# A two-layer decoder trunk: the feed-forward and the second mixer begin by tile of tokens, and the norm's scale and shift move to VectorE

## The chip, the core and the metric

The kernel runs on one core of a Trainium2 chip. The core's engines run side by side and wait for each other through semaphores: TensorE (PE, matrix products; PEld is its weight loading), VectorE (DVE), ScalarE (ACT), GpSimd (POOL), and SyncE (SP), which here only issues DMAs. Each engine takes its instructions strictly in the order in which they are written. The metric is device time in microseconds (us) of one execution. The profile below is of one execution; its times are counted from its first instruction.

## What is computed

256 tokens with 1024 features pass through two layers. Cut to what matters here, the reference is

```python
for l in range(2):
    sh1, sc1, g1, sh2, sc2, g2 = split(c_act @ w_ada[l] + b_ada[l])
    h = x * (1.0 + sc1) + sh1
    mix = hybrid_mixer(h, w_in[l], ...)        # four branches, gates, w_out
    x = layer_norm(alpha * x + g1 * mix, ln1_g[l], ln1_b[l])
    h = x * (1.0 + sc2) + sh2
    f = swiglu(h, ...) if l == 0 else moe(h, ...)
    x = layer_norm(alpha * x + g2 * f, ln2_g[l], ln2_b[l])
```

A layer norm is a mean and a variance over the 1024 features of a token, a normalisation, and then a scale and a shift per feature (`ln_g`, `ln_b`). The next sub-layer needs the norm's result in two forms: as `h`, turned so that features lie on the partitions, for the next products; and as `x`, for the next residual sum.

## The kernel before

**Products.** All weights are fp32 and pass through the core once. A weight chunk of 1 MB (128 x 2048 numbers) is fetched by SyncE into one of three `raw` buffers. Each of its halves (128 x 1024) is split: ScalarE copies it into `whi` in the format fp32r (line 303), and VectorE subtracts that copy from the raw half into `wlo` (line 306). There are five buffers of each. The moving side is split in the same way (`hhi`, `hlo`), and every product is made of three: hi times hi (line 383), lo times hi (384), hi times lo (385). `half` writes the work of one weight half: it splits up to three halves ahead, finishes earlier results (`flush`), writes the products and then lets one step of the side work run (`step`, on the list `tasks`; the heads of the mixer, for instance, are such tasks). The order in which the program is written is the order on each engine; there is no other scheduler.

**Two joints.** There are two places where a layer norm stands between two sub-layers and the kernel goes straight on with products of the result: in layer 0 between the mixer's last projection (`project`) and the feed-forward (`ffn`), called **joint 1** here, and between the feed-forward's second matrix and layer 1's mixer, called **joint 2**. The 256 tokens are two tiles of 128, `x[0]` and `x[1]` ("tile 0" and "tile 1"). `by_token` writes the last four weight halves ahead of a joint so that tile 0 is finished first: its 512 remaining columns (part 0), then tile 1's in two quarters of 256 (parts 1 and 2, woven). After each part `ln_last` writes the sums and the norm's statistics (`ln_part`), and behind the last of a tile the normalisation in place (`ln_fin`, two VectorE instructions at line 542 after a power on GpSimd at line 535).

**What `ln_last` does at the end.** All behind part 2: TensorE turns tile 0 (`transposes`, line 565), then come the two products of a gate row (`row_end`, line 496), then tile 1's turns. `modulate` makes `h` out of the turned tile: eight ScalarE instructions with scale and shift (line 574), the split's copy by ScalarE for tile 0 (line 580) and by VectorE for tile 1 (line 578), and VectorE's subtraction (line 581). Only then `ffn` or the mixer writes its first products, and each of them streams both tiles (256 columns of `h`).

**Scale and shift.** After that `ln_affine` writes four GpSimd instructions of 128 x 1024 (lines 590 and 591) which bring `x` to its final form, with rows that a GpSimd-issued DMA has spread over the partitions. `x` is next read at the next residual sum, many weight halves later.

Layer 1's mixer begins with the chunks of `xbc` (for the state-space branch), then takes the list `PLAN`, in which `bv` is third. `EXTRA` names halves after which one more step of the side work runs.

## Time and profile before

| | |
|---|---|
| time, median of 3 runs | 1923.5 us (1922.97 to 1925.78) |
| the profiled execution's own time | 1922.38 us |
| its span, first to last instruction | 1920.6 us |
| TensorE busy | 1864.4 us, 97% of the span |
| VectorE, ScalarE, GpSimd busy | 1603.2, 1191.6 and 211.5 us |
| layer 0's mixer, joint 1, feed-forward | to 370.9, 370.9 to 410, 410 to 568.7 us |
| joint 2, layer 1's mixer, its projection, experts | 568.7 to 600, 600 to 925, 925 to 942, 942 to 1900 us |

TensorE is the busy engine, so time is gained where it stands still or runs at the lower of its two clocks; the busy time of other engines matters only where TensorE ends up waiting for them. Matrix products overlap in the engine, so a product's row shows a duration that is longer than the distance to the next row; the distance is the cost.

### The profile page before, as it was taken

How to read it: one execution, taken by the hardware profiler on the slowest of the kernel's cores; microseconds unless marked ns; L12 is line 12 of the kernel's file. 1: busy time of each engine (PE TensorE's matmuls, PEld its weight loads, DVE VectorE, ACT ScalarE, POOL GpSimd, SP SyncE). 2: the span in 40 equal slices, each digit the busy share in tenths (PEclk: the TensorE clock that was granted, in tenths of full speed). 3: DMA queues.
4: the chain of work that ended last, by engine and by line, in shares of the span. 5: the costliest groups of instructions: out<-in, count | busy, mean ns of one | idle time of the engine just before them, and what ended most of it. 6: DMA issues, size and time to landing. Idle time of an engine off the chain costs nothing.

```text
span 1920.6 us, 29039 instructions
## 1 busy us (share of the span) xinstructions
PE 1864.4 (97%) x11206; PEld 1629.3 (85%) x11206; DVE 1603.2 (83%) x1995; ACT 1191.6 (62%) x1505; POOL 211.5 (11%) x209
## 2 busy tenths in 40 slices
PE   6999999999999999999999999999999999999997
PEld 5888989899989889999888888888888888888885
DVE  7776876887757686766898998999989999899997
ACT  4546534545435446444577777777777777777774
POOL 0023332110003133321000000000000000000000
PEclk9999999999999999999999999999999999999999
DMA  9565665477845465655899999999999999999992
GB/s 354 190 256 207 233 228 216 153 276 277 302 153 202 160 231 213 237 203 181 337 370 346 345 371 376 380 378 353 369 375 383 378 351 371 349 406 384 381 403 110
DMA packets 86740, 566.00 MB, mean 295 GB/s; under 512 B 10177, under 2 KB 10433, under 8 KB 24642
## 3 DMA queue, kind: packets, MB, share of 16 engines
q1 hardware_dynamic: 82226, 550.30, 75.9%
q0 software_dynamic: 4224, 13.65, 2.0%
q8 instruction: 90, 1.47, 0.3%
q14 instruction: 56, 0.46, 0.1%
q10 hardware_dynamic: 144, 0.11, 0.0%
HBM read 557.21 MB, written 6.82 MB: 294 GB/s over the span
## 4 chain that ended last, share of the span: by engine, by line
PE 89%; DVE 4%; issue 2%; DMA 2%; ACT 1%; POOL 1%; SPq 0%; DVEq 0%; POOLq 0%; ACTq 0%
PE mm L383 22%; PE mm L385 22%; PE mm L384 22%; PE mx L384 6%; PE mx L385 6%; PE mx L383 6%; PE mx L1446 1%; DVE wlo L306 1%; DMA raw<-in_win_dram 1%; PE mx L667 1%; PE mx L1313 1%; ACT h L574 1%; DMA w<-in_cst_dram 1%; DMA raw<-in_adaT_dram 1%; DVE raw L439 0%
## 5 line engine op out<-in xcount | busy, mean ns | idle before, releaser
L306 DVE TENSOR_TENSOR wlo<-raw,whi 128x1024 fp32r<-128x1024 f32 (+1 forms) x880 | 1047.2, 1233 | 196.9 <-ACT whi L303 195.1
L303 ACT ACTIVATE whi<-raw 128x1024 fp32r<-128x1024 f32 (+1 forms) x880 | 879.9, 1051 | 136.1 <-DMA raw<-in_win_dram 29.9
L383 PE MATMUL mm<-hhi,whi 128*128 128x256 f32 x1376 | 393.3, 286 | 16.4 <-ACT whi L303 12.7
L385 PE MATMUL mm<-hhi,wlo 128*128 128x256 f32 x1376 | 386.7, 281 | 7.8 <-DVE wlo L306 7.7
L384 PE MATMUL mm<-hlo,whi 128*128 128x256 f32 x1376 | 386.5, 281 | 0.5 <-DVE hlo L581 0.3
L383 PE MATMUL mm<-whi,ghi 128*128 128x512 f32 x896 | 350.3, 391 | 0.0
L385 PE MATMUL mm<-whi,glo 128*128 128x512 f32 x896 | 349.0, 390 | 0.0
L384 PE MATMUL mm<-wlo,ghi 128*128 128x512 f32 x896 | 348.7, 389 | 0.0
L383 PEld LDWEIGHTS mm<-hhi,whi 128*128 128x128 f32 x1376 | 264.0, 192 | 25.4 <-ACT whi L303 14.8
L385 PEld LDWEIGHTS mm<-hhi,wlo 128*128 128x128 f32 x1376 | 263.8, 192 | 8.7 <-DVE wlo L306 8.7
L384 PEld LDWEIGHTS mm<-hlo,whi 128*128 128x128 f32 x1376 | 264.0, 192 | 1.6 <-DVE hlo L581 1.0
L385 PEld LDWEIGHTS mm<-whi,glo 128*128 128x128 f32 x896 | 168.2, 188 | 35.9
L384 PEld LDWEIGHTS mm<-wlo,ghi 128*128 128x128 f32 x896 | 168.2, 188 | 34.9 <-DVE wlo L306 0.2
L383 PEld LDWEIGHTS mm<-whi,ghi 128*128 128x128 f32 x896 | 168.2, 188 | 34.3
L383 PE MATMUL mx<-whi,ehi 128*128 128x512 f32 x448 | 179.6, 401 | 0.0
L385 PE MATMUL mx<-whi,elo 128*128 128x512 f32 x448 | 175.1, 391 | 0.0
L384 PE MATMUL mx<-wlo,ehi 128*128 128x512 f32 x448 | 174.9, 390 | 0.0
L392 ACT ACTIVATE ehi<-mx 128x512 fp32r<-128x512 f32 x56 | 33.6, 600 | 112.9 <-PE mx L1446 112.9
L1406 POOL DMA_INDIRECT outs<-lnt,row x14 | 14.3, 1025 | 807.0 <-DVE lnt L1400 804.9
L385 PEld LDWEIGHTS mx<-whi,elo 128*128 128x128 f32 x448 | 84.0, 188 | 18.0
L384 PEld LDWEIGHTS mx<-wlo,ehi 128*128 128x128 f32 x448 | 84.3, 188 | 16.5 <-DVE wlo L306 0.8
L383 PEld LDWEIGHTS mx<-whi,ehi 128*128 128x128 f32 x448 | 84.2, 188 | 15.7
(359 smaller groups left out, 2456.1 us busy)
## 6 DMA issues: line engine op xcount, KB each, us to landing
raw<-in_egu_dram SPq DMA_DIRECT2D x205, 1024.0 KB, 7.4
raw<-in_edn_dram SPq DMA_DIRECT2D x96, 1024.0 KB, 7.5
raw<-in_win_dram SPq DMA_DIRECT2D x79, 1024.0 KB, 4.9
raw<-in_adaT_dram SPq DMA_DIRECT2D x31, 1024.0 KB, 5.3
raw<-in_fgu_dram SPq DMA_DIRECT2D x22, 1024.0 KB, 4.9
raw<-in_adaR_dram SPq DMA_DIRECT2D x16, 1024.0 KB, 4.9
raw<-in_wbr_dram SPq DMA_DIRECT2D x16, 1024.0 KB, 4.9
raw<-in_fdn_dram SPq DMA_DIRECT2D x11, 1024.0 KB, 5.8
```

The costliest lines, as they stand in the source:

```text
L303: act.activation(hi[:, c], raw, AF.Copy)
L306: dve.tensor_sub(lo[:, c], raw, hi[:, c].bitcast(F32))
L383: pe.matmul(ps, a[0], b[0], start=start, stop=False, **kw)
L384: pe.matmul(ps, a[0], b[1], start=False, stop=False, **kw)
L385: pe.matmul(ps, a[1], b[0], start=False, stop=stop, **kw)
L392: act.activation(hi, src, AF.Copy)
L574: act.activation(h32[:, j], pts[kh][:, j * 128:(j + 1) * 128], AF.Identity, scale=A[:, k:k + 1], bias=B[:, k:k + 1])
L667: pe.matmul(o[64 * j:64 * j + 64, :], v[:, 0, 128 * p + 64 * j:128 * p + 64 * j + 64], ws[j][:, 0:256], start=True, stop=False, skip_group ...
L1313: pe.matmul(o, xs[t][part][:, k * P:(k + 1) * P], dsp[:, t].rearrange("p a b -> p (a b)"), start=(n == 0), stop=(n == 3))
L1406: nc.gpsimd.indirect_dma_start(outs[c][:, :], bass.IndirectOffsetOnAxis(ap=row[:, 0:1], axis=0), y, None)
L1446: pe.transpose(pt[:, k * P:(k + 1) * P], g[:, k * P:(k + 1) * P], ident)
```

## The change

Before, the order behind a joint was: finish both tiles' norm, turn both, make both tiles of `h`, then products of both. The change interleaves the tiles.

- `by_token` splits one more weight half early, and `ln_last` turns tile 0 ahead of the last twelve products (part 2), and writes tile 0's `modulate` behind part 1.
- The buffers of `h` at joint 1 are new (`h1`), because the old ones still hold the projection's input at that time.
- Tile 1 is normalised by one ScalarE instruction of 128 x 1024 (scale and bias per token) instead of two on VectorE.
- The feed-forward's first pair of chunks and layer 1's `bv`, which becomes the mixer's first projection, go through `token_first`: 24 products of 512 columns for tile 0, then 24 for tile 1, with the four weight halves kept for both. Tile 1's turns stand between tile 0's second and third weight half (`rest`).
- The feed-forward's first pair of chunks is packed the other way round (tokens on the partitions), so its result is turned back by two transposes for each tile.
- `ln_affine` becomes a task: eight VectorE instructions of 128 x 512 in steps of the side work, in layer 0 among the feed-forward's halves, in layer 1 behind all other tasks of the mixer. The GpSimd instructions are gone; GpSimd still issues the DMAs of the rows.

```diff
+    o["fgu"][0:2] = gu[:, :, :, :, 0].transpose(0, 2, 1, 3, 4, 5).reshape(2, P, 2048)
...
+            add(win[i] for i in WIN_N["bv"][0])
             add(win[i] for q in WIN_T["xbc"] for i in q)
...
+                if hold:
+                    assert h == 0 and len(src) == 1
+                    held.append(lambda: dve.tensor_sub(lo, raw, hi.bitcast(F32)))
+                else:
+                    dve.tensor_sub(lo[:, c], raw, hi[:, c].bitcast(F32))
...
+    def token_first(fs, rest, end):
+
+        q = state["done"]
+        for i in range(4):
+            split_upto(q + i)
+            flush()
+            split_upto(q + 3)
+            for f in fs(0, i, *parts[q + i]):
+                f()
+            next(rest, None)
+            step()
+        end(0)
+        for i in range(4):
+            flush()
+            for f in fs(1, i, *parts.pop(q + i)):
+                f()
+            state["done"] += 1
+            split_upto(q + 4 + i)
+            step()
+        end(1)
...
+                if i == 0 and early:
+                    split_upto(q + HALVES)
...
-    def ln_last(pss, grow, AB):
+    def ln_last(pss, grow, AB, new):
+
+        R = {}
+
+        def rest(row, mv):
+            next(row)
+            yield
+            m = modulate(R["hT"], 1, transposes(1), *AB)
+            for _ in m:
+                pass
+            yield
 
         def end(part):
             ln_part(pss[part], grow, *PART[part])
-            if part != 1:
-                ln_fin(PART[part][0])
-            if part == 2:
-                hT = state["hT"] = new_hT()
-                modulate(hT, 0, transposes(0), *AB)
-
+            if part == 0:
+                ln_fin(0)
+            elif part == 1:
+                R["hT"] = state["hT"] = new()
+                R["m"] = modulate(R["hT"], 0, transposes(0), *AB)
+                next(R["m"])
+                split_upto(state["done"] + HALVES - 1, hold=True)
+                next(R["m"])
+            else:
                 row = state.pop("row")
                 next(row)
-                modulate(hT, 1, transposes(1), *AB)
-                next(row)
+                mv = ln_stat(1)
+                dve.scalar_tensor_tensor(mv[:, 4:5], mv[:, 0:1], -1.0, mv[:, 3:4], op0=ALU.mult, op1=ALU.mult)
+                act.activation(x[1], x[1], AF.Identity, scale=mv[:, 3:4], bias=mv[:, 4:5])
+                held.pop()()
+                for _ in R["m"]:
+                    pass
+                state["rest"] = rest(row, mv)
         return end
...
-    def ln_affine(g, b):
-        for t in range(2):
-            pool.tensor_tensor(x[t], x[t], g, op=ALU.mult)
-            pool.tensor_tensor(x[t], x[t], b, op=ALU.add)
+    def ln_affine(l, i, wait=0):
+
+        for _ in range(wait):
+            yield
+        for j, op in ((i, ALU.mult), (i + 1, ALU.add)):
+            cl = [slice(c * 512, (c + 1) * 512) for c in range(2)]
+            rows = [rowp.tile([P, 512], F32, name="lnt", bufs=2) for _ in range(2)]
+            for cs, row in zip(cl, rows):
+                nc.gpsimd.dma_start(row, I["lnp"][l, j:j + 1, cs].to_broadcast([P, 512]))
+            yield
+            for cs, row in zip(cl, rows):
+                yield
+                for t in range(2):
+                    dve.tensor_tensor(x[t][:, cs], x[t][:, cs], row, op=op)
+                    for _ in range(min(wait, 2)):
+                        yield
...
+    def first_N(a, rest, end):
+        pss = [bank() for _ in range(2)]
+        token_first(lambda t, i, hi, lo: [mm3(pss[t], sub(a, A_, 2 * i + k, slice(t * 128, t * 128 + 128)),
+                                              sub((hi, lo), A_, slice(k * 512, (k + 1) * 512)),
+                                              i == 0 and k == 0, i == 3 and k == 1) for k in range(2)],
+                    rest, lambda t: end(pss, t))
...
+        if l == 1:
+            tasks.append(ln_affine(0, 2))
...
+            T["bv"] = proj_N("bv", state.pop("rest"))
...
+        first_N(hT, state.pop("rest"), first)
+        for f2 in range(1, nf // 2):
...
+                h = fp.tile([P, 112 + 4096 + 16], F32R, name="h1")[:, 112:112 + 4096].rearrange("p (i k t) -> p i k t", i=2, k=8)
+                return h[:, 0], h[:, 1]
...
-                ln_affine(lnrow(l, 0, fp), lnrow(l, 1, fp))
+                tasks.append(ln_affine(l, 0, 8))
                 ffn(hT, fp, after_ffn)
...
-WFF = 2, 2
+WFF = 3, 2
-EXTRA = (24, 44, 45, 46), (46, 56)
+EXTRA = (24, 44, 45, 46), (38, 42, 46, 52, 56, 72)
```

The order on three engines at joint 1 follows, before and after (line numbers of the changed kernel are its own; its products stand at lines 417 to 419 and its splits at 310 and 317). First TensorE, from the last products of the projection to the first of the feed-forward; `cst` is the identity matrix of the turns, `x_87` and `x_88` are tiles 0 and 1, `acc` and `one` make the gate row. Before:

```order
L383 MATMUL mx<-whi,hhi 128x256
L384 MATMUL mx<-wlo,hhi 128x256
L385 MATMUL mx<-whi,hlo 128x256
L565 MATMUL mx<-cst,x_87 128x128 x8
L496 MATMUL mx<-acc,one 128x512 x2
L565 MATMUL mx<-cst,x_88 128x128 x8
L383 MATMUL mm<-hhi,whi 128x256
L384 MATMUL mm<-hlo,whi 128x256
L385 MATMUL mm<-hhi,wlo 128x256
```

After (twelve products stand behind the first turns, and twelve between the gate row and the second):

```order
L617 MATMUL mx<-cst,x_87 128x128 x8
L417 MATMUL mx<-whi,hhi 128x256
L418 MATMUL mx<-wlo,hhi 128x256
...
L530 MATMUL mx<-acc,one 128x512 x2
L417 MATMUL mm<-whi,h_3996 128x512
L418 MATMUL mm<-wlo,h_3996 128x512
...
L617 MATMUL mx<-cst,x_88 128x128 x8
```

Tile 0's turns moved ahead of the projection's last twelve products, and tile 1's moved behind the feed-forward's first twelve.

Next ScalarE at the same place; `h_...` are the modulated tiles on their way, `grow` is the gate row. Before:

```order
L303 ACTIVATE whi<-raw 128x1024 x6
L574 ACTIVATE h_4024<-mx,b0B,b0A 128x128 x4
L580 ACTIVATE hhi<-h_4024 128x4x128
L574 ACTIVATE h_4031<-mx,b0B,b0A 128x128 x4
L580 ACTIVATE hhi<-h_4031 128x4x128
L574 ACTIVATE h_4053<-mx,b0B,b0A 128x128 x4
L574 ACTIVATE h_4060<-mx,b0B,b0A 128x128 x4
L501 ACTIVATE grow<-mx 128x512 x2
L303 ACTIVATE whi<-raw 128x1024 x5
```

After:

```order
L626 ACTIVATE h_4007<-mx,b0B,b0A 128x128 x4
L632 ACTIVATE h_3996<-h_4007 128x4x128
L310 ACTIVATE whi<-raw 128x1024
L626 ACTIVATE h_4017<-mx,b0B,b0A 128x128 x4
L632 ACTIVATE h_3996<-h_4017 128x4x128
L605 ACTIVATE x_88<-x_88,lmv 128x1024
L310 ACTIVATE whi<-raw 128x1024
L535 ACTIVATE grow<-mx 128x512 x2
L626 ACTIVATE h_4086<-mx,b0B,b0A 128x128 x4
L626 ACTIVATE h_4093<-mx,b0B,b0A 128x128 x4
L1217 ACT_TABLE_LOAD
```

Two weight copies, tile 1's normalisation and the gate row now stand between the two tiles' modulations.

Last GpSimd, from joint 1's power (`lmv`) to the next layer's accumulator. Before:

```order
L535 TENSOR_TENSOR lmv<-lmv,nhalf 128x1 x2
L585 DMA lnrow<-in_lnp_dram 128x1024 x2
L590 TENSOR_TENSOR x_87<-x_87,lnrow 128x1024
L591 TENSOR_TENSOR x_87<-x_87,lnrow 128x1024
L590 TENSOR_TENSOR x_88<-x_88,lnrow 128x1024
L591 TENSOR_TENSOR x_88<-x_88,lnrow 128x1024
```

After:

```order
L569 TENSOR_TENSOR lmv<-lmv,nhalf 128x1 x2
L646 DMA lnt<-in_lnp_dram 128x512 x4
L506 MEMSET acc 128x1024
L508 DMA acc<-in_bada_dram 1x16x64
L569 TENSOR_TENSOR lmv<-lmv,nhalf 128x1 x2
```

The four large instructions are gone from GpSimd; joint 2's power is five rows away.

## Rows read from the trace of the kernel before

**Rows 1.** Windows by stage: length, busy us (instructions) by engine, granted clock, DMA.

```profile
370.89:410.00 39.11, 32.13 (x228) 29.99 (x227) 34.01 (x41) 21.20 (x37) 14.46 (x9) 0.87 0.55 197
410.00:568.66 158.66, 158.66 (x1195) 150.77 (x1194) 114.08 (x147) 69.17 (x94) 0.56 (x1) 1.00 0.71 257
600.00:925.00 325.00, 322.11 (x2494) 297.12 (x2493) 239.36 (x376) 159.84 (x238) 76.11 (x68) 1.00 0.58 212
```

**Rows 2.** Timeline of TensorE, joint 1: start, us, instruction, count, idle before and releaser.

```profile
366.81 0.28 PE L383 MATMUL mm<-whi,hhi 128*128 128x256 f32 x1
...
372.25 1.03 PE L565 MATMUL mx<-cst,x 128*128 128x128 f32 x8
373.12 1.88 PE L496 MATMUL mx<-acc,one 128*128 128x512 f32 x4
...
379.02 0.38 PE L383 MATMUL mm<-hhi,whi 128*128 128x256 f32 x1 [1.86 <-DVE hhi L578]
...
388.38 0.58 PE L385 MATMUL mm<-hhi,wlo 128*128 128x256 f32 x1 [3.90 <-DVE wlo L306]
```

**Rows 3.** Timeline of TensorE, joint 2.

```profile
562.91 0.28 PE L383 MATMUL mm<-whi,fhi 128*128 128x256 f32 x1
...
568.66 1.03 PE L565 MATMUL mx<-cst,x 128*128 128x128 f32 x8
...
584.78 0.42 PE L385 MATMUL mm<-hhi,wlo 128*128 128x256 f32 x1 [2.99 <-DVE wlo L306]
```

**Rows 4.** Timeline of VectorE, joint 1.

```profile
362.20 1.21 DVE L306 TENSOR_TENSOR wlo<-raw,whi 128x1024 fp32r<-128x1024 f32 x1
...
370.26 1.00 DVE L542 TENSOR_SCALAR x<-x,lmv 128x512 f32<-128x512 f32 x2 [0.67 <-POOL lmv L535]
...
372.45 0.42 DVE L522 TENSOR_TENSOR lnt<-mx,grow 128x256 f32<-128x256 f32 x1
...
374.93 1.00 DVE L542 TENSOR_SCALAR x<-x,lmv 128x512 f32<-128x512 f32 x2 [0.68 <-POOL lmv L535]
...
378.54 0.43 DVE L578 CAST hhi<-h 128x512 fp32r<-128x512 f32 x1 [0.70 <-ACT h L574]
...
384.97 7.81 DVE L306 TENSOR_TENSOR wlo<-raw,whi 128x1024 fp32r<-128x1024 f32 x3
```

**Rows 5.** Instructions that read `lnrow`, whole run: ns min/median/max, first and last start.

```profile
L590 POOL TENSOR_TENSOR x<-x,lnrow x4: 2384/2772/2802, 379.2 to 580.9; 128x1024 f32<-128x1024 f32 x4
L591 POOL TENSOR_TENSOR x<-x,lnrow x4: 2464/2855/3243, 382.0 to 583.7; 128x1024 f32<-128x1024 f32 x4
```

**Rows 6.** Timeline of ScalarE, joint 1 to the first result of the feed-forward.

```profile
372.89 1.51 ACT L574 ACTIVATE h<-mx,b0B,b0A 128x128 f32<-128x128 f32 x4 [10.08 <-PE mx L565]
374.43 0.63 ACT L580 ACTIVATE hhi<-h 128x512 fp32r<-128x512 f32 x1
...
379.75 1.12 ACT L501 ACTIVATE grow<-mx 128x512 f32<-128x512 f32 x2
380.70 3.00 ACT L303 ACTIVATE whi<-raw 128x1024 fp32r<-128x1024 f32 x3
...
399.19 0.38 ACT L1147 ACTIVATE fg<-mm 128x256 f32<-128x256 f32 x1
```

**Rows 7.** Timeline of ScalarE, joint 2, second result of the mixer's first unit.

```profile
594.64 0.60 ACT L699 ACTIVATE pad<-mm 128x512 f32<-128x512 f32 x1 [0.26 <-PE mm L385]
```

**Rows 8.** Windows of TensorE alone: length, busy us (instructions), granted clock, DMA.

```profile
82.00:83.00 1.00, 0.00 (x0) 1.00 0.00 0
286.00:288.00 2.00, 0.39 (x1) 1.00 1.00 332
288.00:290.00 2.00, 1.27 (x5) 0.51 0.92 385
```

**Rows 9.** Timelines of VectorE and of GpSimd behind joint 2.

```profile
589.10 2.35 DVE L306 TENSOR_TENSOR wlo<-raw,whi 128x1024 fp32r<-128x1024 f32 x2
...
589.42 0.54 POOL L1188 DMA_DIRECT2D outs<-lnt  x1
```

## What I predict, and why

> **What bounds the kernel now.** I read the busy times first: TensorE works almost through the whole span, so only its pauses and slow stretches are to be had. The windows by stage say where these are: the feed-forward proper has no pause at all, layer 1's mixer has 2.9 us in 325, and joint 1 has 7 us of idle time in 39 at a mean granted clock of 0.87, that is with a stretch at the lower of its two levels, 1.2 instead of 2.4 GHz [rows 1]. Then I read joint 1 on TensorE's timeline. The reader is to see three things there: tile 0's turns begin at 372.25 right behind the last product, the first product of the feed-forward begins only at 379.02, waiting for VectorE's copy of tile 1's `h`, and 26 products later there is a pause of 3.9 us for a `wlo` [rows 2]. Joint 2 has the same shape, with 3.0 us [rows 3].
>
> Why `wlo` is late is seen on VectorE: alone, the subtraction takes 1.21 us; the three that begin at 384.97 take 7.81, or 2.6 each [rows 4]. In that time GpSimd works on its four scale-and-shift instructions of 2.4 to 3.2 us (eight in the run, four behind each joint) [rows 5]. So each joint pays for a serial chain (norm, turn, modulate, for both tiles) and for VectorE being slowed beside GpSimd.
>
> **How much is to be had.** A product of 256 columns costs 0.113 us (48 from 366.81 to 372.25 [rows 2]), one of 512 twice that, 0.23. The first unit behind joint 1 is 96 products of 256 columns, 10.9 us; with turns (0.87 twice, 372.25 to 373.12) and gate row (1.88) [rows 2] that is 14.5 us of work. It ran from 372.25 to 398.9 (ScalarE takes its last result at 399.19, 0.3 later [rows 6]), or 26.6 us. Joint 2: 568.66 [rows 3] to 594.4 [rows 7], 25.7 us. So 12.1 and 11.2 us are lost, 23.3 in all. This is the most that the change can give at the joints.
>
> **Joint 1 after the change, step by step.** Nothing moves before tile 1's first quarter is done, twelve products before 372.25, at 370.9.
>
> TensorE: `x[0]` is normalised in two instructions from 370.26 [rows 4], so the turns run 370.9 to 371.8, the last twelve products to 373.15, the gate row to 375.05.
>
> ScalarE begins 0.64 after the turns, as it did (372.25 to 372.89 [rows 2, 6]): four modulations 371.55 to 373.05 (1.51), copy to 373.7 (0.63), a weight copy to 374.7 (1.0), four modulations to 376.2, copy to 376.8 [rows 6].
>
> VectorE: behind `x[0]` at 371.2 the early `wlo` to 372.4, then tile 1's first quarter, three steps of 0.46, to 373.8; tile 0's first `hlo`, 512 wide (0.7, from 1.21 for 1024), to 374.5; second quarter, aggregate and GpSimd's power as before 2.5 us (372.45 to 374.93 [rows 4]), to 377.0; one small product more, 377.1; the held `wlo` to 378.3; `hlo` to 379.0.
>
> Tile 1 is normalised on ScalarE from 377.15 to 378.2 (1.05, the price of a 1024-wide copy). Then a weight copy to 379.25 and the gate row, 1.12 [rows 6], to 380.4.
>
> TensorE has tile 0's first twelve products at hand at 375.05 and is through at 377.8. It waits 0.5 us for `x[1]`, turns it until 379.2, and does the other twelve by 381.95 (the last `wlo` is there at 380.5). Tile 1's modulations are done by 381.9 and 383.4 on ScalarE, the copies and subtractions on VectorE (0.43 [rows 4] and 0.7) at 382.4, 383.1, 383.9, 384.6. TensorE waits another 0.5 and 0.2 us and then runs 24 products with a turn of tile 0's result (0.2) to 388.4.
>
> So the unit ends at 388.4 instead of 398.9: **10.5 us**, less 0.2 for the second turn-back, **10.3**. What hides the chain is tile 0's own products: if they weren't there, tile 1's modulations from 380.4 would all stand on the path. What is late next is ScalarE, unbroken from 371.55 to 383.4, and then the table load. Behind it the weight copies for the next unit are ready at 386 and 387, in time for 388.4, and the chunk for the fourth one is fetched when the second is split, at about 388.6, eleven us ahead of its products at about 399.5.
>
> **Joint 2.** The same steps from 567.2 (twelve products of 0.12 us before 568.66 [rows 3]). No turn-back is needed, `bv` is wanted with tokens on the partitions. With the same 17.5 us the unit ends at 584.7 instead of 594.4: **9.7 us**.
>
> **Scale and shift.** GpSimd's eight instructions go, and with them VectorE's slow stretches, already counted above. VectorE gets 16 instructions of 512 columns, 0.7 us each or 5.6 us per layer. In the feed-forward it is busy 114 of 158.7 us and in the mixer 239 of 325 [rows 1]; at the rate of one or two per weight half (2.7 us of products) they fit. They wait for rows fetched by GpSimd's queue, and behind them on VectorE the next `wlo` is queued; but the rows are asked for at least one half ahead. I put this at 0; if each stood on the path it would be 11.2 us.
>
> **The rest.** Layer 1's mixer starts `xbc` four halves later, and its tasks get eight steps more. I put that at 0, between -2.9 (all its idle time gone) and the price of the second rival.
>
> A rule bears on joint 2. Beside a DMA issue of GpSimd, two subtractions took 2.35 us [rows 9], no more than alone. The Trainium skill, "SBUF — State Buffer", section "Who interferes with whom", says that a copy or cast on VectorE can enter a two-port mode that holds a port pair shared with GpSimd, and that whichever comes second waits for the whole of the other. The change puts the eight clearing DMAs of the mixer close to tile 1's two casts; by the rule each cast could wait for one issue (0.54 us [rows 9]), and joint 2 would give 8.6 instead of 9.7 us. No run here shows a cast there, and I leave it out.
>
> **Sum.** 10.3 + 9.7 = 20.0 us. I take off 1 us for some twenty hand-overs between engines that I rounded away: 19.0. The profiled execution took 1922.4 us (span 1920.6), 1.1 below the median of 1923.5; against the median this gives **1904.5 us**. A measurement of this kernel can tell about 0.2%, 3.8 us, from no change.
>
> **Rivals.**
> *The clock falls at the joints all the same.* Against it: a pause of 1.1 us left the clock at its upper level [rows 8], and mine are 0.5. For it: with 0.39 us of work between 286 and 288 it fell [rows 8], and turns and gate row stand close to my pauses. Joint 1's mean of 0.87 over 39 us is 10 us at half speed, 5 us lost [rows 1]; kept at both joints, 10 us: 1914.5. Chance 0.10.
>
> *A branch in layer 1's mixer isn't ready.* The state-space and stick-breaking heads begin four halves later (4 x 2.7 = 10.9 us); if the added steps don't make up for that, `flush_to` writes their remaining steps without products between them, and TensorE pauses. At most the whole delay comes back: 1915. For it: the heads are long chains through four engines. Against: idle time there is only 2.9 us now [rows 1], and eight steps are added for six used. Chance 0.09.
>
> *The place of `h1`.* Products cost 0.113 us in the projection, but 48 of them cost 5.75 us, 0.120 each, with `fhi` [rows 2, 3]: where the operands lie seems to matter. The feed-forward streams `h1` in 960 products; at 0.120 it would lose 6.2 us: 1910.7, chance 0.05. This is also how it ends slower: from 0.139 us on (20.0 + 3.8 us over 960 products) the change costs more than it gives. At 0.142, a quarter above the dearest row here, 1930 us. No row has such a price; chance 0.02.
>
> *The change does nothing.* Tile 1's chain could be so late that TensorE waits for it as before. It would have to lose 17 of 20 us, four times the ScalarE chain between 377 and 381. Chance 0.04; 1922.
>
> **How the numbers follow.** My own case has 0.70: from 1900 (the full 23.3 us) to 1909 (two us more lost at each joint). The range goes on to 1912.5 to take in a clock that falls at one joint only, and the mild form of the third rival; outside stay the first two rivals at full price, the last two cases, and little below. Faster by over 0.2%: 0.94; within: 0.04; slower: 0.02.
>
> **What would show it.** Right: no TensorE pause above 1 us at either joint; granted clock at 1.00 through both; no VectorE subtraction of 1024 columns above 1.3 us there; the end of the first unit 17 to 18 us after tile 1's first quarter. Wrong: a wait for `x[1]` or tile 1's `h` of 2 us or more; half clock behind 382; pauses in layer 1's mixer above 5 us; products of the feed-forward at 0.12 us apart.

## The result, and the profile after

The changed kernel takes 1905.5 us (median of 4 runs, 1901.95 to 1908.61) against 1924.3 for the kernel before: a ratio of 0.9902, 95% interval 0.9885 to 0.9919. Run twice more beside the kernel before, it gave 0.9894 (0.9876 to 0.9913) and 0.9893 (0.9873 to 0.9913), with medians of 1904.3 and 1902.7 us. So it is about 1% faster; forecast were 1904.5 us, between 1900 and 1912.5. The execution behind the first profile took 1908.6 us (span 1906.6), the slowest of its four.

One view carries most of what follows: windows that cut the program at the same five points in every kernel: where tile 1's first quarter is done (joint 1 begins), the first product behind the first unit, a pair of weight chunks (joint 1 ends), the same two points at joint 2, and the last turns of layer 1. Columns: window, its length, busy us (instructions) of TensorE, its weight loads, VectorE, ScalarE and GpSimd, TensorE's granted clock, DMA share, GB/s. The rows are joint 1, feed-forward, joint 2, layer 1's mixer. The kernel before:

```profile
370.89:398.99 28.10, 21.12 (x130) 18.98 (x129) 24.43 (x28) 15.66 (x29) 14.46 (x9) 0.82 0.39 140
398.99:567.23 168.24, 168.24 (x1281) 160.35 (x1280) 122.36 (x157) 74.70 (x103) 0.56 (x1) 1.00 0.73 265
567.23:594.45 27.22, 21.36 (x131) 19.08 (x130) 21.61 (x23) 15.21 (x29) 16.96 (x17) 0.81 0.43 137
594.45:923.41 328.96, 326.07 (x2528) 301.08 (x2527) 243.99 (x384) 162.94 (x242) 76.19 (x69) 1.00 0.59 214
```

The changed kernel, first profile:

```profile
372.39:389.74 17.35, 16.89 (x85) 12.85 (x84) 13.33 (x23) 16.28 (x30) 1.66 (x3) 1.00 0.44 151
389.74:562.18 172.44, 172.44 (x1281) 164.52 (x1280) 127.07 (x169) 75.72 (x103) 3.14 (x5) 1.00 0.74 266
562.18:579.41 17.23, 16.67 (x83) 12.66 (x81) 13.85 (x23) 15.32 (x28) 5.66 (x12) 1.00 0.70 246
579.41:908.76 329.35, 326.16 (x2576) 304.30 (x2575) 246.18 (x389) 162.96 (x244) 72.79 (x72) 1.00 0.59 211
```

The joints fell from 28.10 and 27.22 us to 17.35 and 17.23, and the granted clock there rose from 0.82 and 0.81 to 1.00: 20.74 us gained. The span fell by only 14.0 us (1920.57 to 1906.61). The rest is in the other rows: the feed-forward took 4.20 us more although TensorE never paused in it, the mixer 0.39 more; joint 1 began 1.50 us later (between 369.85 and 372.39 in the three traces of the changed kernel), and the part behind the mixer took 0.69 more. 10.75 + 9.99 - 4.20 - 0.39 - 1.50 - 0.69 = 13.96.

Joint 1 on TensorE, to be held against [rows 2]:

```profile
372.39 1.09 PE L617 MATMUL mx<-cst,x 128*128 128x128 f32 x8
...
374.74 1.88 PE L530 MATMUL mx<-acc,one 128*128 128x512 f32 x4
376.05 0.79 PE L417 MATMUL mm<-whi,h 128*128 128x512 f32 x1
...
379.84 1.09 PE L617 MATMUL mx<-cst,x 128*128 128x128 f32 x8 [0.46 <-ACT x L605]
...
383.61 0.50 PE L417 MATMUL mm<-whi,h 128*128 128x512 f32 x1
```

In [rows 2] the first product of the feed-forward came at 379.02, 6.8 us behind the start of tile 0's turns, and a wait of 3.90 us followed. Now products of tile 0 start 3.7 us behind it, the only wait listed in the joint is 0.46 us for tile 1's norm, and tile 1's products begin at 383.61. VectorE's copy and subtraction for the second half of tile 1, which took 2.30 and 2.78 us while GpSimd worked on scale and shift, take 0.43 and 0.69; those for the first half took 0.43 and 0.69 in both. Before:

```profile
379.93 2.30 DVE L578 CAST hhi<-h 128x512 fp32r<-128x512 f32 x1 [0.24 <-ACT h L574]
382.27 2.78 DVE L581 TENSOR_TENSOR hlo<-h,hhi 128x512 fp32r<-128x512 f32 x1
```

After, with a weight subtraction ahead of them:

```profile
380.77 1.23 DVE L317 TENSOR_TENSOR wlo<-raw,whi 128x1024 fp32r<-128x1024 f32 x1 [0.51 <-ACT whi L310]
...
384.53 0.43 DVE L630 CAST h<-h 128x512 fp32r<-128x512 f32 x1 [0.24 <-ACT h L626]
384.99 0.69 DVE L635 TENSOR_TENSOR h<-h,h 128x512 fp32r<-128x512 f32 x1
```

### The profile page after: what moved, and what is told of

It reads as the page before. It is cut to its first block, busy times and chain, and to the rows that moved or that the text cites. A ratio compares the mean times of both kernels' runs of the same rounds, so it can differ in the third digit from the quotient of the medians.

```text
span 1906.6 us, 28966 instructions
## 1 busy us (share of the span) xinstructions
PE 1862.5 (98%) x11162; PEld 1627.6 (85%) x11162; DVE 1592.1 (84%) x2009; ACT 1194.6 (63%) x1507; POOL 186.6 (10%) x205
## 4 chain that ended last, share of the span: by engine, by line
PE 92%; DVE 3%; DMA 2%; issue 1%; ACT 1%; POOL 0%; SPq 0%; DVEq 0%; ACTq 0%; POOLq 0%
PE mm L417 23%; PE mm L419 22%; PE mm L418 22%; PE mx L419 6%; PE mx L418 6%; PE mx L417 6%; PE mx L1540 1%; DMA raw<-in_win_dram 1%; PE mx L1407 1%; DMA raw<-in_adaT_dram 1%; PE mx L739 1%; DVE wlo L317 1%; DVE raw L473 0%; PE mx L963 0%; DVE a L781 0%
## 5 line engine op out<-in xcount | busy, mean ns | idle before, releaser
L317 DVE TENSOR_TENSOR wlo<-raw,whi 128x1024 fp32r<-128x1024 f32 (+1 forms) x878 | 1036.4, 1223 | 188.8 <-ACT whi L310 187.1
L417 PE MATMUL mm<-hhi,whi 128*128 128x256 f32 x1024 | 293.1, 286 | 14.0 <-ACT whi L310 14.0
L419 PE MATMUL mm<-hhi,wlo 128*128 128x256 f32 x1024 | 286.4, 280 | 0.9 <-DVE wlo L317 0.9
L418 PE MATMUL mm<-hlo,whi 128*128 128x256 f32 x1024 | 286.3, 280 | 0.0
L417 PEld LDWEIGHTS mm<-hhi,whi 128*128 128x128 f32 x1024 | 194.4, 190 | 22.6 <-ACT whi L310 16.4
L419 PEld LDWEIGHTS mm<-hhi,wlo 128*128 128x128 f32 x1024 | 194.5, 190 | 1.4 <-DVE wlo L317 1.4
L418 PEld LDWEIGHTS mm<-hlo,whi 128*128 128x128 f32 x1024 | 194.5, 190 | 0.7 <-issue 0.5
```

What stands on the lines that cost most here:

```text
L317: dve.tensor_sub(lo[:, c], raw, hi[:, c].bitcast(F32))
L417: pe.matmul(ps, a[0], b[0], start=start, stop=False, **kw)
L418: pe.matmul(ps, a[0], b[1], start=False, stop=False, **kw)
L419: pe.matmul(ps, a[1], b[0], start=False, stop=stop, **kw)
```

## The experiments

All times of whole kernels below are medians, all ratios against the kernel before on the same chip.

### Where did 4 us in the feed-forward come from?

Both kernels once more with a trace, unchanged.

> The changed kernel as it is, once more with a trace, and five rounds against the kernel before. In the first trace the two joints took 17.35 and 17.23 us (28.0 and 27.2 before), but the products of the feed-forward went at 0.1178 us apart from 397.9 on, where those of the kernel before went at 0.1133; that alone is 4.1 us between the joints. Theory (the pace of products is a level that is taken up when the stream is broken by other instructions, and then holds): joints again within 0.3 us of 17.3; the feed-forward at 0.113 or 0.118 and not necessarily the same as in the first trace; time 1901 to 1909. Rival (the pace belongs to the place of h1): 0.1178 again from the same product on, and the feed-forward again 172.4 us from the end of its first unit to joint 2.

> The kernel before, once more with a trace. Theory of the level of pace: the feed-forward's 864 products may go at 0.113 or 0.118 us; the joints again 28 and 27 us. Rival (the place of the operand): 0.1133 again throughout the feed-forward.

> The changed kernel as it is, for comparison with the next two on the same chip. Joints 17.3 and 17.2 us, 2.1 us of wait at the retention heads' second pair in layer 1's mixer, 329 to 331 us from the end of joint 2's first unit to the mixer's last turns, the feed-forward at one or the other pace; time 1901 to 1908.

The feed-forward's row of the kernel before (second trace), and of the changed kernel (second and third trace):

```profile
399.31:571.83 172.52, 172.52 (x1281) 164.62 (x1280) 122.22 (x157) 74.55 (x102) 0.56 (x1) 1.00 0.71 258
```

```profile
387.19:559.63 172.44, 172.44 (x1281) 164.52 (x1280) 127.08 (x169) 75.53 (x103) 3.14 (x5) 1.00 0.75 266
```

```profile
389.43:557.91 168.48, 168.48 (x1281) 160.59 (x1280) 127.08 (x169) 76.12 (x103) 3.13 (x5) 1.00 0.77 272
```

Each kernel shows both lengths: 168.24 and 172.52 before, 172.44 twice and 168.48 after. The groups of instructions from 402 to 482 us say what differs (columns: count, then busy us and mean ns of one). The kernel before, first trace, then second trace:

```profile
L385 PE MATMUL mm<-hhi,wlo 128*128 128x256 f32 x236 | 65.1, 276 | 0.0
```

```profile
L385 PE MATMUL mm<-hhi,wlo 128*128 128x256 f32 x227 | 63.8, 281 | 0.0
```

Three groups of this size alternate. In the same 80 us 236 products of each ran, or 227: a product every 0.113 or every 0.118 us, at a granted clock of 1.00 both times. The second trace of the changed kernel by itself came out as the rival had it, with 172.44 us again; the other two traces speak against it. `h1` is not the cause, since the kernel before has no `h1` and shows the slower pace, and the changed kernel has it and shows the faster. The joints agree to 0.02 us in the three traces of the changed kernel. In the second trace of the kernel before they took 28.33 and 28.44 us, so the joints gave 20.7 to 22.2 us. Traces with the same pace differ by 20.0 us in their spans (1920.6 and 1900.5) and by 22.2 (1926.4 and 1904.2). Median times of 1904.3 and 1902.7 us stand in the range that was expected; the third trace's mixer, 327.49 us, lies below the 329 to 331 that were.

### Scale and shift alone

The kernel before, with `ln_affine` as a task on VectorE and the extra steps, the tiles in the old order.

```diff
+        if l == 1:
+            tasks.append(ln_affine(0, 2))
...
-                ln_affine(lnrow(l, 0, fp), lnrow(l, 1, fp))
...
+                tasks.append(ln_affine(l, 0, 8))
...
-                ln_affine(lnrow(l, 2, fp), lnrow(l, 3, fp))
...
-EXTRA = (24, 44, 45, 46), (46, 56)
+EXTRA = (24, 44, 45, 46), (38, 42, 46, 52, 56, 72)
```

> The kernel before, with the scale and shift alone moved to VectorE tasks (16 instructions of 512 columns, and the extra steps); the tiles stay in the old order. Theory (half of what the joints lost was VectorE beside GpSimd): the first product of the feed-forward still begins near 379 with a wait of 1.9 us for tile 1's h and the clock still falls there, but the cast takes 0.43 and the subtraction 0.7 to 1.2 us, the wait of 3.9 us for wlo is gone and with it the second stretch at half clock; the first unit ends at 392 instead of 398.9, joint 2's at about 588.5 instead of 594.4: 12 to 13 us in all, 1911. Rival (the order of the tiles is all that counts, wlo is late because VectorE gets to it late): the wait for wlo stays above 2.5 us and the time at 1919 to 1923.

1912.0 us, ratio 0.9934 (0.9912 to 0.9956). Its four windows, and VectorE at joint 1:

```profile
373.17:394.51 21.34, 18.26 (x131) 16.31 (x129) 16.26 (x27) 14.97 (x28) 1.81 (x3) 0.92 0.45 164
394.51:562.75 168.24, 168.24 (x1281) 160.36 (x1280) 126.75 (x165) 75.55 (x104) 3.14 (x5) 1.00 0.74 267
562.75:583.14 20.39, 17.03 (x131) 14.88 (x130) 13.58 (x23) 15.13 (x29) 4.99 (x11) 1.00 0.59 220
583.14:910.31 327.17, 325.50 (x2529) 301.48 (x2528) 251.45 (x392) 163.32 (x242) 70.65 (x73) 1.00 0.59 213
```

```profile
382.22 0.43 DVE L578 CAST hhi<-h 128x512 fp32r<-128x512 f32 x1 [0.24 <-ACT h L574]
382.68 0.69 DVE L581 TENSOR_TENSOR hlo<-h,hhi 128x512 fp32r<-128x512 f32 x1
384.14 3.50 DVE L306 TENSOR_TENSOR wlo<-raw,whi 128x1024 fp32r<-128x1024 f32 x3 [0.77 <-ACT whi L303]
```

The theory holds: three subtractions take 3.50 us in place of 7.81 [rows 4], and the wait of 3.90 us for `wlo` is gone. The granted clock fell at joint 1, to a mean of 0.92, as expected; at joint 2 it stayed at 1.00, which wasn't. The joints give 6.8 us each, 13.6 of the 20.7, with the tiles in the old order. The interleaving then adds 7.1 (21.34 to 17.35 and 20.39 to 17.23). That this split depends on which part comes first is seen in the next section.

### Interleaving with GpSimd still doing scale and shift

Two ways. First, written behind each joint:

```diff
             next(rest, None)
             step()
+            if i == 2:
+                ln_affine(0, 2 * (state["mix"] > 0))
...
-                    dve.tensor_tensor(x[t][:, cs], x[t][:, cs], row, op=op)
+                    pool.tensor_tensor(x[t][:, cs], x[t][:, cs], row, op=op)
```

> The changed kernel, but scale and shift are done by GpSimd again, eight instructions of 128 x 512 behind each joint, written where tile 1's turned tile is made. Theory (GpSimd's work slows VectorE's casts and subtractions by two to four times): tile 1's cast and subtraction take 2 us and more, TensorE waits 3 to 8 us for tile 1's h at each joint, and 8 to 14 of the 20.6 us that the joints gave are lost: 1911 to 1919. Rival (with the tiles interleaved nothing waits for VectorE any more, so the engine of scale and shift does not matter): joints at 17 to 18.5 us, 1904 to 1908.

1919.1 us, ratio 0.9971 (0.9958 to 0.9983): at the upper edge of what the theory expected, but not for its reason. The joints came out as the rival had them. Joint 1 and the mixer:

```profile
371.13:389.55 18.42, 16.93 (x84) 12.84 (x83) 15.31 (x23) 16.82 (x30) 6.92 (x7) 1.00 0.42 142
...
575.13:916.97 341.84, 328.85 (x2575) 306.42 (x2574) 243.24 (x384) 162.51 (x244) 84.28 (x85) 0.98 0.58 208
```

Joint 1 lost 1.1 us, joint 2 nothing (17.06 us; GpSimd's first scale came behind tile 1's copies there); over 11 us were lost in the mixer. GpSimd, VectorE and TensorE there show how:

```profile
595.25 2.47 POOL L647 TENSOR_TENSOR x<-x,lnt 128x512 f32<-128x512 f32 x2 [2.94 <-DMA lnt<-in_lnp_dram]
597.68 2.71 POOL L1274 DMA_DIRECT2D outs<-lnt  x5
600.37 0.16 POOL L764 MEMSET pad<- 128x6 f32 x2
```

```profile
600.53 1.67 DVE L775 SCALAR_TENSOR_TENSOR a<-pad,sm,a 128x256 f32<-128x256 f32 x4 [13.31 <-POOL pad L764]
```

```profile
604.18 0.58 PE L421 MATMUL mm<-hhi,wlo 128*128 128x256 f32 x1 [9.61 <-DVE wlo L317]
```

The convolution's small clear of `pad` is written behind scale and shift on GpSimd's queue, which waited for rows between each pair of instructions. VectorE waited 13.31 us for the clear with the next `wlo` queued behind it, and TensorE 9.61 us for that. This loss is one of queue order, which my experiment made itself. So a second one leaves the tasks as they are and changes the engine alone:

```diff
-                    dve.tensor_tensor(x[t][:, cs], x[t][:, cs], row, op=op)
+                    pool.tensor_tensor(x[t][:, cs], x[t][:, cs], row, op=op)
```

> The changed kernel with the scale and shift still in the same steps of the side work, but done by GpSimd (16 instructions of 128 x 512 in place of VectorE's). It tells the engine apart from the place: with GpSimd behind the joint 15 us were lost, 12 of them because the convolution's clears of pad stood behind the scale and shift on GpSimd's queue. Theory (GpSimd's work costs only where VectorE or a later GpSimd instruction has no slack): subtractions of VectorE beside it take up to 2.5 us, but TensorE waits no more in the feed-forward, joints at 17.2 to 17.6 us, time 1902 to 1909. Rival (VectorE beside GpSimd is too slow anywhere, so the engine is the point): TensorE waits for wlo in the feed-forward and behind the mixer's heads, 1912 or more.

1907.7 us, ratio 0.9914 (0.9897 to 0.9931). Joint 1, and GpSimd and VectorE in it:

```profile
369.79:389.19 19.40, 16.98 (x85) 12.85 (x83) 16.70 (x23) 16.97 (x30) 8.91 (x10) 1.00 0.48 162
```

```profile
379.26 5.64 POOL L651 TENSOR_TENSOR x<-x,lnt 128x512 f32<-128x512 f32 x4 [2.47 <-PE mx L617]
```

```profile
380.51 1.57 DVE L630 CAST h<-h 128x512 fp32r<-128x512 f32 x1 [1.14 <-ACT h L626]
382.11 1.65 DVE L635 TENSOR_TENSOR h<-h,h 128x512 fp32r<-128x512 f32 x1
383.68 1.51 DVE L630 CAST h<-h 128x512 fp32r<-128x512 f32 x1
```

The time is as the theory had it, the joint is not: 19.40 us in place of 17.2 to 17.6. The task is written among later halves, but GpSimd had nothing queued ahead of it and started at 379.26, once tile 1's turns had read `x`, right beside tile 1's copies, which take 1.5 us in place of 0.43. In the changed kernel VectorE's queue holds the first of these instructions back to 397.89. So on this engine the place in the program did not set the time, and the price of GpSimd as the engine is 2.1 us at joint 1. At joint 2 (17.17 us) it wasn't tested: the task stands behind all others of the mixer there and began at 869.59. The mixer took 331.71 us, 1.5 to 4.2 more than in the three traces of the changed kernel.

This run also shows the split the other way round. With the tiles interleaved and GpSimd still doing scale and shift, joint 1 fell from 28.10 to 19.40 us, 8.7 of the 10.75, and the kernel gained 16.1 us (1923.9 to 1907.7); with scale and shift moved alone joint 1 gained 6.8 and the kernel 11.9. Each part alone takes away much of the same loss: scale and shift off GpSimd make tile 1's chain short, and interleaving puts tile 0's products beside it.

A rule of the Trainium skill, "SBUF — State Buffer", section "Who interferes with whom", says that a VectorE instruction with two inputs in SBUF contends with a GpSimd instruction that reads SBUF. The traces agree: the subtraction of two SBUF operands takes 2.6 us beside GpSimd [rows 4], and 1.23 in the changed kernel.

### The 16 VectorE instructions, and who normalises tile 1

Scale and shift left out, with the DMAs of their rows:

```diff
-                nc.gpsimd.dma_start(row, I["lnp"][l, j:j + 1, cs].to_broadcast([P, 512]))
...
-                    dve.tensor_tensor(x[t][:, cs], x[t][:, cs], row, op=op)
```

> The changed kernel without the 16 scale and shift instructions and without the DMAs of their rows: x is not scaled and shifted behind layer 0's norms, so this part of the computation is left out. Theory (they cost nothing, as the prediction had it): joints at 17.3 us, TensorE's waits in the feed-forward and in layer 1's mixer as in the changed kernel, time 1901 to 1908. Rival (each of 0.7 us stands on the path): up to 11 us less, 1893 to 1898.

1901.7 us, ratio 0.9888 (0.9871 to 0.9904), joints 17.31 and 17.23 us, feed-forward and mixer:

```profile
386.76:555.27 168.51, 168.51 (x1281) 160.62 (x1280) 122.30 (x161) 75.61 (x103) 0.56 (x1) 1.00 0.74 269
...
572.50:903.11 330.61, 327.44 (x2576) 305.61 (x2575) 241.76 (x383) 162.93 (x244) 69.65 (x68) 0.99 0.58 208
```

168.51 us without the instructions and 168.48 with them at the same pace; the mixer is no shorter either (330.61 against 327.49 to 330.24). No row shows a cost, and the ratio's interval overlaps those of the changed kernel, whose lowest ratio is 0.9893.

Tile 1 normalised on VectorE:

```diff
-                dve.scalar_tensor_tensor(mv[:, 4:5], mv[:, 0:1], -1.0, mv[:, 3:4], op0=ALU.mult, op1=ALU.mult)
-                act.activation(x[1], x[1], AF.Identity, scale=mv[:, 3:4], bias=mv[:, 4:5])
+                ln_fin(1, mv)
```

> The changed kernel, but tile 1 is normalised by two VectorE instructions (1.0 us) in place of one on ScalarE (1.24 us). Theory (ScalarE is what is latest behind tile 1's norm, and VectorE has the room): TensorE's wait of 0.5 us for x of tile 1 goes, ScalarE's modulations of tile 1 begin 0.7 us sooner, joints at 17.0 to 17.3 us, time 1902 to 1907. Rival (VectorE's held subtraction and tile 0's second hlo are late by the microsecond that it works longer): TensorE waits 0.5 to 1.5 us for one of them after tile 1's turns, joints at 17.8 to 18.5 us, time 1905 to 1909.

1906.4 us, ratio 0.9914 (0.9897 to 0.9930), feed-forward at the slower pace (172.73). The joints are shorter than the changed kernel's:

```profile
371.63:388.62 16.99, 16.87 (x84) 13.07 (x83) 15.09 (x26) 15.50 (x29) 1.81 (x3) 1.00 0.49 158
...
561.35:578.12 16.77, 16.48 (x83) 12.79 (x81) 14.51 (x24) 14.06 (x27) 5.77 (x12) 1.00 0.70 228
```

The theory holds: 0.36 and 0.46 us less, and no wait for tile 1's norm. (Two later runs with the same norm gave 16.91 and 16.89 us at joint 1, 16.80 and 16.78 at joint 2.) This part of the change, the norm on ScalarE, costs 0.8 us; that is too little to see in the total time.

### One break less

The first pair's result is kept and turned back ahead of the last pair, so that nothing stands between products from joint 1 to there.

```diff
+            if f2 == nf // 2 - 1:
+                evacs.extend(back)
```

> The changed kernel, but the first pair's result is kept in buffers of its own and is turned back for both tiles just ahead of the last pair of the feed-forward, so that nothing breaks the stream of products between the end of joint 1 and there. Theory (the pace is a level that the stream falls into where other instructions break it; behind joint 1 it was at 0.113 in both traces of the changed kernel, until tile 1's turn-back): 0.113 us apart through to the last pair, the feed-forward 3.5 to 4 us shorter, 1899 to 1903. Rival (the pace is a matter of time or of the operand): 0.118 from some 26 us behind tile 0's turns on, as before, 1903 to 1906.

1904.2 us, ratio 0.9897 (0.9881 to 0.9914), feed-forward 172.54 us: the number of the theory failed, the slower pace was there from the end of joint 1. But it ended at the turn-back, at 491.74. Ten microseconds on either side of it:

```profile
481.00:491.00 10.00, 10.00 (x87) 10.00 (x86) 7.23 (x10) 5.00 (x8) 0.00 (x0) 1.00 0.85 313
493.00:503.00 10.00, 10.00 (x91) 10.00 (x90) 7.65 (x12) 4.96 (x7) 0.00 (x0) 1.00 0.86 312
```

87 products touch the first window and 91 the second. The rival failed too: the slower pace was there 17 us behind the start of tile 0's turns and not only after 26, and the faster products behind the turn-back read the same `h1`. In the first and second trace of the changed kernel the distance rose from 0.113 to 0.118 us at tile 1's turn-back; in the third it stayed at 0.113 there. So in these traces a pace holds until other instructions break the stream, and can change either way there. What decides it isn't known.

### What joint 2 gives, and what is given back

Joint 1 as changed, joint 2 and the mixer's order as before (`old_last` writes a joint's end in the old order):

```diff
-            add(win[i] for i in WIN_N["bv"][0])
...
-            T["bv"] = proj_N("bv", state.pop("rest"))
...
-                by_token(lambda p, i, hi, lo: fs(p, both + i, hi, lo), ln_last(pss, modrow[0, 1], nxt(), new_hT), True)
+                by_token(lambda p, i, hi, lo: fs(p, both + i, hi, lo), old_last(pss, modrow[0, 1], nxt(), new_hT))
```

> The changed kernel, but joint 2 and the start of layer 1's mixer in the old order (both tiles' norm, both turned, then xbc with products of both tiles; bv third again); scale and shift stay VectorE tasks. Theory (each joint stands for itself, and the new order of layer 1's first projections costs nothing): joint 1 at 17.3 us, joint 2 at 20.3 us as with scale and shift moved alone, from there to layer 1's last turns as with scale and shift moved alone (327.2 us), time 1905 to 1910. Rival (bv ahead of xbc delays the state-space branch, so that joint 2's 3 us are given back in the mixer): the stretch behind joint 2 is 3 us shorter than the changed kernel's 329.4 to 330.2, time 1902 to 1906.

1905.6 us, ratio 0.9901 (0.9882 to 0.9920). Joint 1 took 17.33 us, joint 2 and the mixer:

```profile
558.13:579.34 21.21, 18.14 (x130) 16.19 (x129) 13.57 (x23) 15.11 (x29) 4.91 (x11) 0.92 0.62 221
579.34:906.68 327.34, 325.55 (x2529) 301.45 (x2528) 250.91 (x392) 163.10 (x242) 72.04 (x73) 1.00 0.59 213
```

Joint 2 is 4.0 us longer than the changed kernel's, but the mixer is 2.0 us shorter (327.34 against 329.35; the other two traces of the changed kernel have 330.24 and 327.49, so more than one thing varies there). The length less TensorE's busy time varies less: 1.79 us idle here and 1.67 with scale and shift moved alone, against 3.19, 4.05 and 3.08 in the three traces of the changed kernel. The waits of TensorE in the mixer (in total, times, longest), changed kernel and this one:

```profile
PE mx L1077 <- DVE w L1071: 2.1, 1, 2.1
PE mx L843 <- DVE sp L839: 1.1, 1, 1.1
```

```profile
PE mx L856 <- DVE sp L852: 1.1, 1, 1.1
PE mx L1039 <- POOL w L1033: 0.6, 1, 0.6
```

In the changed kernel one wait is new, 2.0 to 2.2 us in all three traces: retention's second pair of heads. GpSimd and VectorE there (`w` are its decay rows, `rmv` the first pair's statistics):

```profile
802.66 1.96 POOL L1089 TENSOR_TENSOR rmv<-rmv,nhalf 128x4 f32<-128x4 f32 x1 [2.99 <-DVE rmv L1088]
804.58 1.14 POOL L1061 DMA_DIRECT2D w<-in_cst_dram  x2
```

```profile
809.24 1.04 DVE L1071 TENSOR_TENSOR w<-mx,w 128x384 f32<-128x384 f32 x2 [3.22 <-DMA w<-in_cst_dram]
```

The rows are asked for only at 804.58, behind the first pair's statistics; the products written ahead of this step end at 807.6, and TensorE stands. With `bv` third this request was at 791.66, and TensorE did not wait for it. So theory and rival were each half right: joint 1 took the same 17.3 us with the old joint 2, and of joint 2's gain (3.2 to 4.0 us) the mixer gives back 1.3 to 2.4 us of idle time, with the late head as the new wait that all three traces share. The total time can't tell: 1905.6 us here, 1902.7 to 1905.5 for the changed kernel.

I tried to get that part back, with tile 1's norm on VectorE and more steps of the side work, early or late in the mixer:

```diff
-EXTRA = (24, 44, 45, 46), (38, 42, 46, 52, 56, 72)
+EXTRA = (24, 44, 45, 46), (26, 30, 34, 38, 42, 46, 52, 56, 72)
```

```diff
-EXTRA = (24, 44, 45, 46), (38, 42, 46, 52, 56, 72)
+EXTRA = (24, 44, 45, 46), (38, 42, 46, 52, 56, 60, 64, 72)
```

> Tile 1 normalised on VectorE, and three more steps of the side work early in layer 1's mixer (after halves 26, 30 and 34). In the changed kernel the second pair's decay rows are asked for on GpSimd's queue only behind a power that waits for the first pair's statistics, 4.7 us ahead of their use; with bv as third projection they were asked for 3 us sooner and ahead of the gates. Theory (2 us of what joint 2 gains are given back by this wait, since the heads begin four halves later): with the steps earlier the wait is under 0.3 us, the stretch 327.0 to 328.5 us, joints 16.8 to 17.0, time 2.5 to 3.5 us below the changed kernel's on the same chip. Rival (the stretch is longer because of the pace of products or for other reasons): the wait may go, but the stretch stays at 329 to 331.

> Tile 1 normalised on VectorE, and two more steps of the side work late in layer 1's mixer (after halves 60 and 64): the heads' second pair comes two halves earlier, but its decay rows are still asked for between two instructions of the first pair's on GpSimd. Theory: the wait of 2.1 us shrinks to 0 to 1 us, the stretch to 327.5 to 329 us. Rival (as above): 329 to 331 us.

Both failed: 1905.3 us (0.9900, 0.9881 to 0.9920) and 1910.0 us (0.9926, 0.9906 to 0.9946), the changed kernel on the same chip 1902.7. The mixer took 332.29 and 332.10 us. The early steps moved the request for the second pair's rows to 791.53, but the pair came sooner too and still waited 1.3 us, and other heads waited as well; the late ones made two waits of one. TensorE's waits with the early steps, then with the late ones:

```profile
PE mx L962 <- POOL w L931: 2.1, 3, 1.2
PE mx L1076 <- DVE w L1070: 1.3, 1, 1.3
...
```

```profile
PE mx L1076 <- DVE w L1070: 3.6, 2, 2.2
...
```

So no version that does the whole work beat the changed kernel. That the lost 2 us can be won with the steps in other places wasn't shown.

## Why the prediction was right, and where its steps were off

**Joint 1.** Right to 0.15 us: 17.35 us were measured from tile 1's first quarter to the end of the first unit, 17.5 forecast. Counted from that point, tile 1's first product began at 11.2 us (11.55 in the forecast); ScalarE, with one gap of 0.30 us where the forecast had none, was through with tile 1's modulations at 12.1 (forecast 12.5); the wait for tile 1's norm was 0.46 (0.5). Single prices were off: ScalarE's norm of tile 1 took 1.24 us, for which the forecast had taken a copy's 1.05.

**Joint 2.** 17.23 us against 17.5. The wait for GpSimd's DMA issues that was left out would have cost up to 1.1 us; the first of tile 1's copies, beside the end of GpSimd's last clearing DMA, took 0.54 us in place of 0.43, in all three traces 0.53 or 0.54. So 0.1 us, and leaving it out was right here. What a copy would pay in the midst of those DMAs isn't shown: only their last 0.3 us lay beside it.

**The allowance of 1 us** for hand-overs is a term that was mis-sized: the joints gave 20.7 to 22.2 us, more than the 20.0 before the allowance. The steps had been rounded up enough already.

**Scale and shift at 0:** no row shows a cost when they are left out. But the forecast booked GpSimd's part inside the joints and never split it off. The parts don't add: with the tiles in the old order, moving scale and shift gives 13.6 of the 20.7 us at the joints; with the tiles interleaved first, it is worth 2.1 us at joint 1.

**Layer 1's mixer at 0** was right in sum (327.49 to 330.24 us against 328.96 and 329.05), from parts that the forecast didn't have. The second rival came in a small form: one head is late by 2.0 to 2.2 us, in place of the 11 that the rival had as its most. Its steps were right (heads begin four halves later, and at the end the products written ahead of a step run out before it is ready); its size was taken from the whole delay and not from the one head that comes last. Other waits went: with scale and shift moved alone, extra steps included, TensorE was idle there for 1.67 us, against 2.89 and 3.09 in the two traces of the kernel before. The changed kernel's 3.08 to 4.05 us are the two effects together.

**The place of `h1`,** the third rival, is refuted by the second trace of the kernel before and the third of the changed one. The observation under it, products at 0.113 and at 0.120 us, is real; and the sign that was to tell of it, products of the feed-forward at 0.12 us apart, nearly showed (0.118) in two of three traces without `h1` being the cause. For 256 columns in the feed-forward there are two paces with 4 us between them, and both kernels have both. The profiled run of before had the faster one and that of the changed kernel the slower, so the first pair of profiles shows 14.0 us where medians differ by 18.8, 19.6 and 23.6. That the number fits to 1 us is partly luck: the pace alone moves a run by 4. Under the same rival the forecast misread a row: 0.142 us is a quarter above 0.113, not above the dearest row (0.120), and gives some 1932 us.

**The clock** stayed at its upper level through both joints in all three traces, with pauses of about 0.5 us; that rival fell.

## What to carry to other kernels

Before a chain is reordered, ask what slows each link: here moving four elementwise instructions off GpSimd gave 13.6 us at the joints with no reordering at all. Do not credit a part of a change from one order of the experiments: taken alone, each of the two parts here removes much of the same loss. GpSimd's queue was often empty (busy 10% of the span), so work "spread out" on it started as soon as its data were there, beside what was critical, and what was queued behind it waited. When two profiles differ in stretches that the change doesn't touch, take a second trace of each kernel before explaining it.

## What the hardware showed that was not expected

**Two paces of the same stream.** Over all traces the feed-forward took either 168.24 to 168.52 us or 172.44 to 172.73, seven of fourteen traces each, with nothing between and a granted clock of 1.00. Products of 256 columns come every 0.113 or every 0.118 us. In one run a pace held over a hundred microseconds of unbroken products, and it changed where other TensorE instructions broke the stream. Both paces were seen on one chip. The pace explains about 4 us of what runs of one kernel differ by. Its cause is open.

**The same waits, a different clock.** With scale and shift moved alone, TensorE waited 0.78, 1.86, 0.34 and later 0.28 us at joint 2 and the granted clock was 1.00; in the kernel that has only joint 1 changed, the waits there were 0.84, 1.86 and 0.34, and the mean clock was 0.92; the joint took 21.21 us against 20.39. Whether the clock falls at such a joint couldn't be read from the order of the work alone in these two traces.
